# A two-layer decoder trunk on one core: U gathers of layer 1 wait for TensorE, and V rows are placed closer together

## The chip, the cores and the metric

The kernel runs on one core of a Trainium2 chip. The metric is the device time of one execution in microseconds (us). The engines are TensorE (PE, with its weight loads as PEld), VectorE (DVE), ScalarE (ACT), GpSimd (POOL) and SyncE (SP). Each engine works through a queue of its own in order; DMAs are issued from the queues of SP and of POOL.

## The reference, cut to what matters

Two layers, each a token mixer (attention in layer 0, a gated short convolution in layer 1) and then a PEER mixer: for each of 512 tokens a router picks 128 experts (8 heads x 16) out of 16384, each expert being a row of `expert_u` and a row of `expert_v`, of 1024 floats.

```python
for i in range(DEPTH):                      # DEPTH = 2, SEQ = 512, D_MODEL = 1024
    h = rmsnorm(x, norm_mix[i])
    x = x + (sliding_window_attention(h, ...) if i % 2 == 0 else short_gated_conv(h, ...))
    h = rmsnorm(x, norm_ffn[i])
    x = x + peer_ffn(h, peer_w_query[i], peer_sub_keys[i], peer_u[i], peer_v[i])
# in peer_ffn: idx, g = the 128 experts of each token and their softmax weights
u = jnp.take(expert_u, ic, axis=0)
a = jnp.einsum('td,thkd->thk', xc, u)
w = gc * jax.nn.gelu(a, approximate=False)
v = jnp.take(expert_v, ic, axis=0)
y = jnp.einsum('thk,thkd->td', w, v)
```

## The kernel before

The 512 tokens are four tiles of 128. In each layer the PEER mixer is computed in two ways at once. Tiles 2 and 3 are **dense**: all 16384 experts go through TensorE in 128 steps of 128 experts. Step `i` has a key half (`ustep`, L704: load 0.5 MB of transposed U rows as `du`, split them into a high part on ACT, `uh`, and a low part on VectorE, `ul`, 24 matmuls by `mm3`, GELU into `dw`) and a value half (`vstep`, L714: `dw` times the routing weights `G`, split into `wh` and `wl`, load 0.5 MB of V rows as `dv`, split into `vh` and `vl`, 12 matmuls into `y`). The key half runs `LAG` = 7 steps ahead; the first 15 key halves come before step 0, so steps 0 to 7 have a value half alone, and steps 121 to 127 too. `gen` (L738) makes `G` for 32 steps and 16 tokens: ACT copies `jr` and `igr`, VectorE compares and multiplies (`oj`, `igr`, `oi`), 32 small matmuls; 16 gens fill one quarter of the steps. The product `dw` x `G` (L717) runs on GpSimd when it is emitted while U rows are being handed out (`st["gu"]`), else on VectorE.

Tiles 0 and 1 are **gathered** (`gather`, L622): for each of 128 expert places a U gather, an indirect DMA of 128 rows (0.5 MB) issued by POOL (L633), then one VectorE reduction against `xn` (L638); then GELU; then 128 V gathers (L666), each with two matmuls into `acc` (L676). The gather buffers are six (two more in front 1), so a gather waits until the reduction, or the matmul, of an older row has let go of a buffer.

Three streams are written out in one order by `merge` (L814), which has a virtual clock: each `yield` of a stream says how far its next piece lies behind. `stream_d` is the spine: attention of tile 0, front 0 (attention of tiles 1 to 3, router), dense 0, front 1 (`conv` for tiles 1 to 3, projection `proj`, router), dense 1. `stream_g` has the gathers, tile by tile: layer 0 tiles 0 and 1, layer 1 tiles 0 and 1. `stream_f` has the small fronts of the gathered tiles. `rate` (L806) is the distance of two gathered rows on that clock, a pair (U rows, V rows): `DR1` in dense 1, `FR1` in front 1, `DR0` and `FR0` in layer 0. A dense step is `DSTEP` = 6.8, a conv piece 5.25. The order of emission is a priority: a scheduler then puts each engine's queue in order, and it lets an instruction that is ready pass older ones that are not. So a row can run long before the place at which it is emitted.

In front 0 a U row also waits for the last matmul of an attention step that was emitted before it: `attn` sets `st["mark"]` (L341), and `gather` makes the DMA depend on it (L635). In layer 1 there is no mark.

Of the kernel before, what the change touches and what calls it, by code (L numbers as in the profile page):

```python
# [19 lines left out]
P = 128  # L20
D = 1024
KC = 8
# [50 lines left out]
WSB = 2  # L73
GX1 = 2

DR0 = (2.4, 2.4)
DR1 = (2.5, 2.5)
FR0 = (2.2, 3.0)
FR1 = (3.0, 3.0)


@with_exitstack
def trunk(ctx: ExitStack, tc: tile.TileContext, a: dict, out: bass.AP):
    nc = tc.nc
# [25 lines left out]
    first = {}  # L110
# [56 lines left out]
    def split(src, pool, tags, bufs):  # L167
        hi = pool.tile([P, KC, P], F32R, name="whi", tag=tags[0], bufs=bufs)
        lo = pool.tile([P, KC, P], F32R, name="wlo", tag=tags[1], bufs=bufs)
        nc.scalar.copy(hi, src)  # L170
        nc.vector.tensor_tensor(lo, src, hi, op=ALU.subtract)
        return hi, lo

    def mm3(ps, w, x, ts):
        for k in range(KC):
            nc.tensor.matmul(ps, w[0][:, k, :], x[0][:, k, ts], start=(k == 0), stop=False)  # L176
            nc.tensor.matmul(ps, w[0][:, k, :], x[1][:, k, ts], start=False, stop=False)  # L177
        for k in range(KC):
            nc.tensor.matmul(ps, w[1][:, k, :], x[0][:, k, ts], start=False, stop=(k == KC - 1))  # L179

    def proj(src, lhs, tiles, psum, sp):
        for h in range(2):
# [169 lines left out]
    def conv(tiles, pool, psum, slow=1.0):  # L352
        n = len(tiles)
        T = n * P
        gain = gain_of(a["norm_mix"][1:2, :])
        c3 = C3 and n > 1
        if c3:
            hh = pool.tile([P, KC, T], F32R, name="hh", tag="hh")
            hl = pool.tile([P, KC, T], F32R, name="hl", tag="hl")
# [3 lines left out]
        for j, t in enumerate(tiles):  # L363
# [6 lines left out]
            if c3:  # L370
                h = b4.tile([P, D], F32, name="h", tag="b4")
                norm(t, gain, h)
                for half in range(2):
                    ps = psum("psT")
# [16 lines left out]
        for c in range(KC):  # L391
            pss = [None] * 3
            cc = pool.tile([P, 3, T + 2], F32, name="cc", tag="cc")
            u, z, v = cc[:, 0, :T], cc[:, 1, :], cc[:, 2, :T]
            for part in (2, 1, 0):
                w = piece(a["w_in"][c, part])
                ps = psum(f"psbcu{part}")
                if c3:
                    mm3(ps[:, :T], split(w, pool, ("wh", "wl"), WSB), (hh, hl), slice(0, T))
                else:  # L400
                    for k in range(KC):
                        nc.tensor.matmul(ps[:, :T], w[:, k, :], hT[:, k, :], start=(k == 0), stop=(k == KC - 1))
                if part == 2:
                    nc.scalar.copy(u, ps[:, :T])
                elif part == 1:
                    nc.vector.tensor_copy(z[:, 0:2], zh[:, c, :])
                    nc.vector.tensor_tensor(z[:, 2:], ps[:, :T], u, op=ALU.mult)
                    nc.vector.tensor_copy(zh[:, c, :], z[:, T:T + 2])
                    nc.scalar.mul(v, z[:, 0:T], convw[:, 0, c:c + 1])
                    for q in (1, 2):  # L410
                        nc.vector.scalar_tensor_tensor(v, z[:, q:T + q], convw[:, q, c:c + 1], v,
                                                       op0=ALU.mult, op1=ALU.add)
                else:
                    y = v if sp else yT[:, c, :]
                    nc.vector.tensor_tensor(y, v, ps[:, :T], op=ALU.mult)
                    if sp:
                        nc.scalar.copy(yh[:, c, :], y)
                        nc.vector.tensor_tensor(yl[:, c, :], y, yh[:, c, :], op=ALU.subtract)
                yield 1.75 * n * slow
# [202 lines left out]
    def gather(l, t, r):  # L622
# [5 lines left out]
        for s in range(P):  # L628
            if early and s % TK == 0:
                yield f"h{l}_{t}_{s // TK}"  # L630
            h, c = divmod(s, TK)
            ug = gtile("ug")
            ld = nc.gpsimd.indirect_dma_start(out=ug, out_offset=None, in_=a[f"u{l}"],  # L633
                                              in_offset=bass.IndirectOffsetOnAxis(ap=r["idx"][h][:, c:c + 1], axis=0))
            if "mark" in st:  # L635
                tc.add_manual_dep(ld.ins, st["mark"], together, reason="pace of the front")
            with tc.high_priority(offset=HPT):
                nc.vector.tensor_tensor_reduce(out=ug, in0=ug, in1=xn, scale=1.0, scalar=0.0, op0=ALU.mult,  # L638
                                               op1=ALU.add, accum_out=act[:, s:s + 1])
            yield rate()  # L640
# [4 lines left out]
        w = s2.tile([P, P], F32, name="wgt", bufs=1)  # L645
# [7 lines left out]
        for gr in range(2):  # L653
            acc = pv.tile([P, 512], F32, name="acc", tag="acc")
            for q in range(4):
# [5 lines left out]
                for r8 in range(8):  # L661
                    vgs = []
                    for j in range(2):
                        tt = 64 * gr + 32 * j + 8 * q + r8
# [7 lines left out]
                    with tc.high_priority(offset=HPF if st.get("front") else HPV):  # L672
                        for j in range(2):
                            for h in range(2):
                                c = 32 * (2 * j + h)
                                mm = nc.tensor.matmul(acc[c:c + 32, :], wd[:, j, r8, :],  # L676
                                                      vgs[j][:, h * 512:(h + 1) * 512],
                                                      start=(q == 0 and r8 == 0), stop=(q == 3 and r8 == 7))
# [13 lines left out]
    def dense(l, rs, pool):  # L692
        ys = [[py(f"y{tt}{h}") for h in range(2)] for tt in range(2)]
# [20 lines left out]
        def vstep(i):  # L714
            first, last = i == 0, i == NK - 1
            w = ws.pop(i)
            (nc.gpsimd if (WPU if st.get("gu") else WPV) else nc.vector).tensor_tensor(w, w, G[:, i % GR, :], op=ALU.mult)  # L717
            f = VU if st.get("gu") else VG if i % IC >= 2 * IC - GR else VB0
            sp = int((i + 1) * f) > int(i * f)
            if sp:  # L720
                wh = pool.tile([P, T2], F32R, name="wh", tag="wh", bufs=2)
                wl = pool.tile([P, T2], F32R, name="wl", tag="wl", bufs=2)
                nc.scalar.copy(wh, w)
                nc.vector.tensor_tensor(wl, w, wh, op=ALU.subtract)  # L724
            v = pool.tile([P, D], F32, name="dv", tag="raw", bufs=RB)
            nc.sync.dma_start(v, a[f"v{l}"][i * P:(i + 1) * P, :])
            if sp:
                vh, vl = halves(v, [P, D], "v")
                terms = ((wh, vh), (wl, vh), (wh, vl))
            else:  # L730
                terms = ((w, v),)
            for k, (x, m) in enumerate(terms):
                for tt in range(2):
                    for h in range(2):
                        nc.tensor.matmul(ys[tt][h], x[:, tt * P:(tt + 1) * P], m[:, h * 512:(h + 1) * 512],  # L735
                                         start=first and k == 0, stop=last and k == len(terms) - 1)

        def gen(i, tg):  # L738
            ijg = rs[tg * TG // P]["ijg"]
# [29 lines left out]
                gen(c * IC, tg)  # L769

        npre = GR - IC
        for i in range(LAG + npre):
            ustep(i)
            yield 1.0
# [3 lines left out]
        for i in range(NK):  # L778
# [7 lines left out]
            vstep(i)  # L786
            yield DSTEP
        st["ys"] = ys

    def finish(l, ys, pool):  # L790
        for tt in range(2):
# [12 lines left out]
    st = {"dense": False, "front": False, "pace": FS0}  # L804

    def rate():  # L806
        u = 0 if st.get("gu") else 1
        if st["dense"]:
            return (DR1 if "f1" in st else DR0)[u]
        if st["front"]:  # L810
# [182 lines left out]
```

## Time and profile before

| | us |
|---|---|
| median of 3 runs | 2992.05 (2991.13 to 2999.46) |
| the profiled execution | 2989.34 |
| its span, first to last instruction | 2987.5 |
| PE busy | 2624.3 (88%) |
| DVE busy | 2246.6 (75%) |
| ACT busy | 1559.3 (52%) |
| POOL busy | 1364.6 (46%) |

A busy time is a mean over stages that have different limits, so the page is read by stages. On the time axis layer 1 lies so: dense 0 ends about 1655 us, conv's matmuls run from 1675 to 1783, the value halves of dense 1 begin about 2085 and end with the program. U rows of tile 0 are gathered from 1512 to 1808, those of tile 1 from 2077 to 2367; V rows of tile 1 until 2732. In the views a line such as `L735` is a line of the kernel; a count such as x444 is a count of instructions; clock is the granted TensorE clock as a share of the full one.

### The profile page before, as it was taken

The page shows a single profiled execution, that of the slowest core. Times are in us where ns is not written, and L with a number is a line of the kernel's source. Part 1 is how long each engine was busy: PE and PEld are TensorE (multiplying, and loading weights), DVE is VectorE, ACT ScalarE, POOL GpSimd, SP SyncE. Part 2 cuts the span into 40 slices and gives each one's busy share as a digit, 9 for nine tenths or more (in the row PEclk, how much of TensorE's full clock was granted, in tenths as well). Part 3 has the DMA queues.
Part 4 walks back from the last instruction along what each step waited for, and adds up shares of the span by engine and source line. Part 5 has one row for each costly group of instructions (what it writes and reads, how often), then busy time and mean ns, then how long its engine had stood idle before and what let it go on. Part 6 is the DMA issues. An engine that isn't in the chain of part 4 may idle for free. (4 is left out here: it accounts for less than half of the span.)

```text
span 2987.5 us, 53454 instructions
## 1 busy us (share of the span) xinstructions
PE 2624.3 (88%) x19980; PEld 2098.1 (70%) x19980; DVE 2246.6 (75%) x5225; ACT 1559.3 (52%) x2384; POOL 1364.6 (46%) x1163
## 2 busy tenths in 40 slices
PE   5966878869999988999998699986788699999999
PEld 5763476626788877777777696763577577777898
DVE  2496699984898899546479995988999946546655
ACT  4226333584773367448343333358356538637644
POOL 0152554464555545434357754446755755541000
PEclk8987889969999999999999799998899899999999
DMA  5883788989999988999999998998999899996554
GB/s 199 291 315 127 253 311 316 338 315 347 333 367 377 395 304 321 340 324 333 337 366 378 364 366 315 320 335 318 357 348 357 309 338 327 345 333 231 175 187 159
DMA packets 263203, 931.37 MB, mean 312 GB/s; under 512 B 29984, under 2 KB 38560, under 8 KB 262944
## 3 DMA queue, kind: packets, MB, share of 16 engines
q0 software_dynamic: 147456, 536.94, 49.5%
q1 hardware_dynamic: 115488, 391.03, 35.9%
q8 instruction: 157, 2.57, 0.3%
q14 instruction: 102, 0.84, 0.1%
HBM read 916.31 MB, written 11.53 MB: 311 GB/s over the span
## 5 line engine op out<-in xcount | busy, mean ns | idle before, releaser
L633 POOL DMA_INDIRECT ug<-in_u_dram,idx x512 | 684.7, 1337 | 669.6 <-DVE act L638 248.9
L666 POOL DMA_INDIRECT vg<-in_v_dram,idxT x512 | 553.7, 1081 | 640.1 <-PE acc L676 511.8
L638 DVE CUSTOM_DVE_ANT_0 ug<-ug,xn 128x1024 f32<-128x1024 f32 x512 | 626.0, 1235 | 40.0 <-DMA ug<-in_u_dram,idx 39.4
L176 PE MATMUL psA<-xh,uh 128*128 128x256 f32 x2048 | 523.4, 292 | 46.7 <-ACT dw L711 20.0
L177 PE MATMUL psA<-xl,uh 128*128 128x256 f32 x2048 | 510.9, 286 | 0.0
L701 DVE TENSOR_TENSOR ul<-du,uh 128x1024 fp32r<-128x1024 f32 x256 | 320.8, 1253 | 202.7 <-ACT uh L700 163.1
L176 PEld LDWEIGHTS psA<-xh,uh 128*128 128x128 f32 x2048 | 395.4, 193 | 104.9 <-ACT dw L711 32.7
L701 DVE TENSOR_TENSOR vl<-dv,vh 128x1024 fp32r<-128x1024 f32 x256 | 318.5, 1245 | 170.1 <-ACT vh L700 166.6
L177 PEld LDWEIGHTS psA<-xl,uh 128*128 128x128 f32 x2048 | 395.9, 193 | 16.4 <-issue 10.5
L700 ACT CAST uh<-du 128x1024 fp32r<-128x1024 f32 x256 | 268.7, 1050 | 204.7 <-PE psA L177 162.4
L700 ACT CAST vh<-dv 128x1024 fp32r<-128x1024 f32 x256 | 268.9, 1051 | 186.5 <-PE y L735 172.9
L676 PE MATMUL acc<-vg,wd 128*32 128x512 f32 x2048 | 290.4, 646 | 35.4 <-DMA vg<-in_v_dram,idxT 32.1
L179 PE MATMUL psA<-xh,ul 128*128 128x256 f32 x2048 | 299.0, 287 | 18.7 <-DVE ul L701 18.7
L735 PE MATMUL y<-vh,wh 128*128 128x512 f32 x1024 | 289.9, 403 | 27.0 <-ACT vh L700 18.4
L179 PEld LDWEIGHTS psA<-xh,ul 128*128 128x128 f32 x2048 | 266.7, 191 | 52.5 <-DVE ul L701 24.7
L735 PE MATMUL y<-vl,wh 128*128 128x512 f32 x1024 | 287.5, 402 | 16.0 <-DVE vl L701 15.7
L735 PE MATMUL y<-vh,wl 128*128 128x512 f32 x1024 | 283.2, 397 | 16.6 <-DVE wl L724 16.5
L742 ACT COPY jr<-ijg 128x2048 f16<-128x2048 f16 x128 | 243.5, 1902 | 50.6 <-DVE oj L746 49.7
L735 PEld LDWEIGHTS y<-vh,wl 128*128 128x128 f32 x1024 | 192.8, 190 | 73.1 <-DVE wl L724 20.8
L735 PEld LDWEIGHTS y<-vl,wh 128*128 128x128 f32 x1024 | 189.1, 191 | 72.4 <-DVE vl L701 21.2
L735 PEld LDWEIGHTS y<-vh,wh 128*128 128x128 f32 x1024 | 178.6, 191 | 73.8 <-ACT vh L700 25.6
L744 ACT COPY igr<-ijg 128x1536 f16<-128x1536 f16 x128 | 188.8, 1475 | 35.3 <-DVE oi L751 34.9
(208 smaller groups left out, 4004.8 us busy)
## 6 DMA issues: line engine op xcount, KB each, us to landing
du<-in_uT_dram SPq DMA_DIRECT2D x256, 512.0 KB, 6.5
dv<-in_v_dram SPq DMA_DIRECT2D x256, 512.0 KB, 6.3
wpc<-in_wq_dram SPq DMA_DIRECT2D x64, 512.0 KB, 6.0
wpc<-in_w_in_dram SPq DMA_DIRECT2D x48, 512.0 KB, 7.1
wpo<-in_wo_dram SPq DMA_DIRECT2D x16, 512.0 KB, 4.5
ug<-in_u_dram,idx POOLq DMA_INDIRECT x512, 7.6
vg<-in_v_dram,idxT POOLq DMA_INDIRECT x512, 7.2
wpo<-in_w_out_dram SPq DMA_DIRECT2D x16, 512.0 KB, 6.7
```

The source lines that it names most:

```text
L176: nc.tensor.matmul(ps, w[0][:, k, :], x[0][:, k, ts], start=(k == 0), stop=False)
L177: nc.tensor.matmul(ps, w[0][:, k, :], x[1][:, k, ts], start=False, stop=False)
L179: nc.tensor.matmul(ps, w[1][:, k, :], x[0][:, k, ts], start=False, stop=(k == KC - 1))
L633: ld = nc.gpsimd.indirect_dma_start(out=ug, out_offset=None, in_=a[f"u{l}"], in_offset=bass.IndirectOffsetOnAxis(ap=r["idx"][h][:, c:c + 1 ...
L638: nc.vector.tensor_tensor_reduce(out=ug, in0=ug, in1=xn, scale=1.0, scalar=0.0, op0=ALU.mult, op1=ALU.add, accum_out=act[:, s:s + 1])
L666: ld = nc.gpsimd.indirect_dma_start(out=vg, out_offset=None, in_=a[f"v{l}"], in_offset=bass.IndirectOffsetOnAxis(ap=idxT[:, tt:tt + 1], ax ...
L676: mm = nc.tensor.matmul(acc[c:c + 32, :], wd[:, j, r8, :], vgs[j][:, h * 512:(h + 1) * 512], start=(q == 0 and r8 == 0), stop=(q == 3 and ...
L700: nc.scalar.copy(hi, w)
L701: nc.vector.tensor_tensor(lo, w, hi, op=ALU.subtract)
L735: nc.tensor.matmul(ys[tt][h], x[:, tt * P:(tt + 1) * P], m[:, h * 512:(h + 1) * 512], start=first and k == 0, stop=last and k == len(terms ...
L742: nc.scalar.copy(jr, ijg[:, 0, t0:t0 + TG].unsqueeze(2).to_broadcast([P, TG, P]))
L744: nc.scalar.copy(igr, ijg[:, 1:4, t0:t0 + TG].unsqueeze(3).to_broadcast([P, 3, TG, IC]))
```

## The change

In conv for tiles 1 to 3, every piece's last matmul becomes the mark. In dense 1 the mark at the time a row is emitted is the last matmul of the value half one step before the one just emitted. So a U gather of layer 1 that is emitted behind the first conv piece waits, on POOL, for the mark that holds at its emission; U rows of tile 0 that are emitted before it have none. V gathers wait for no mark. The distances change too: V rows of dense 1 from 2.5 to 1.8, U rows of front 1 from 3.0 to 3.5, V rows of front 1 from 3.0 to 2.5. U rows of dense 1 stay at 2.5, which is 6.8 / 2.5 = 2.7 rows to a step.

```diff
-DR1 = (2.5, 2.5)
+DR1 = (2.5, 1.8)
-FR1 = (3.0, 3.0)
+FR1 = (3.5, 2.5)
...
 def mm3(ps, w, x, ts):
...
-            nc.tensor.matmul(ps, w[1][:, k, :], x[0][:, k, ts], start=False, stop=(k == KC - 1))
+            mm = nc.tensor.matmul(ps, w[1][:, k, :], x[0][:, k, ts], start=False, stop=(k == KC - 1))
+        return mm.ins.name
...
 def conv(tiles, pool, psum, slow=1.0):
...
-                    mm3(ps[:, :T], split(w, pool, ("wh", "wl"), WSB), (hh, hl), slice(0, T))
+                    st["mark"] = mm3(ps[:, :T], split(w, pool, ("wh", "wl"), WSB), (hh, hl), slice(0, T))
...
 def gather(l, t, r):
...
-            if "mark" in st:
+            if st.get("mark"):
                 tc.add_manual_dep(ld.ins, st["mark"], together, reason="pace of the front")
...
 def dense(l, rs, pool):
     def vstep(i):
...
-                        nc.tensor.matmul(ys[tt][h], x[:, tt * P:(tt + 1) * P], m[:, h * 512:(h + 1) * 512],
-                                         start=first and k == 0, stop=last and k == len(terms) - 1)
+                        mm = nc.tensor.matmul(ys[tt][h], x[:, tt * P:(tt + 1) * P], m[:, h * 512:(h + 1) * 512],
+                                              start=first and k == 0, stop=last and k == len(terms) - 1)
+            if l == 1:
+                st["mark"], st["next"] = st["next"], mm.ins.name
...
         npre = GR - IC
+        st["mark"] = st["next"] = None
         for i in range(LAG + npre):
...
         st["ys"] = ys
+        st["mark"] = st["next"]
```

## Rows read from the trace of the kernel before

**Rows 1.** Windows of dense 1: length, busy us (instructions) of each engine, clock, DMA.
```profile
2085.00:2385.00 300.00, 226.86 (x1662) 188.56 (x1663) 293.86 (x455) 163.80 (x209) 202.88 (x143) 0.91 0.92 340
2385.00:2732.00 347.00, 347.00 (x2767) 258.68 (x2769) 185.92 (x213) 194.25 (x263) 164.48 (x163) 1.00 0.92 330
```
**Rows 2.** The chain that ended last: start us, us, what.
```profile
2389.85 2.71 PE acc L676 x24
...
2943.05 2.77 PE y L735 x12
2948.66 2.77 PE y L735 x12
```
**Rows 3.** Windows of three lines alone: L735 twice, L179 once, L755 twice.
```profile
2085.00:2385.00 300.00, 122.19 (x444) 85.28 (x444) 0.91 0.92 340
2385.00:2732.00 347.00, 140.38 (x552) 98.85 (x552) 1.00 0.92 330
...
2085.00:2385.00 300.00, 33.30 (x232) 30.31 (x232) 0.91 0.92 340
...
2085.00:2385.00 300.00, 15.66 (x512) 14.10 (x512) 0.91 0.92 340
2385.00:2732.00 347.00, 20.16 (x608) 17.17 (x608) 1.00 0.92 330
```
**Rows 4.** Window of tile vg: PE, PEld and POOL; four matmul records to a row.
```profile
2385.00:2732.00 347.00, 66.89 (x508) 10.28 (x512) 126.58 (x122) 1.00 0.92 330
```
**Rows 5.** Windows of the seam and of the projection, columns as in rows 1.
```profile
1597.00:1655.00 58.00, 43.57 (x231) 36.19 (x229) 56.98 (x84) 21.00 (x30) 45.89 (x32) 0.97 0.96 358
1650.00:1675.00 25.00, 5.63 (x24) 4.71 (x24) 23.13 (x41) 7.93 (x15) 16.50 (x14) 0.52 1.01 396
1785.00:1860.00 75.00, 68.16 (x406) 47.72 (x406) 42.08 (x104) 26.56 (x42) 32.85 (x32) 0.95 0.87 320
```
**Rows 6.** Tiles ug, psbcu, vg: duration ns min/median/max, first and last start us.
```profile
L633 POOL DMA_INDIRECT ug<-in_u_dram,idx x68: 933/1234/1987, 1511.7 to 1659.6; - x68
...
L179 PE MATMUL psbcu<-hh,wlo x192: 336/336/339, 1683.4 to 1782.8; 128*128 128x384 f32 x192
...
L676 PE MATMUL acc<-vg,wd x512: 589/617/1064, 1820.5 to 2083.2; 128*32 128x512 f32 x171
```
**Rows 7.** Window of tile ug: DVE and POOL.
```profile
1650.00:1675.00 25.00, 13.45 (x12) 16.50 (x14) 0.52 1.01 396
```
**Rows 8.** Lines of DVE, 2100 to 2340: xcount, busy us, mean ns, idle before.
```profile
L638 DVE CUSTOM_DVE_ANT_0 ug<-ug,xn 128x1024 f32<-128x1024 f32 x108 | 129.3, 1215 | 1.3 <-DMA ug<-in_u_dram,idx 1.3
...
L701 DVE TENSOR_TENSOR ul<-du,uh 128x1024 fp32r<-128x1024 f32 x26 | 31.8, 1224 | 1.4 <-ACT uh L700 1.4
L746 DVE TENSOR_TENSOR oj<-jr,io 128x2048 f16<-128x2048 f16 x14 | 17.2, 1226 | 0.0
L724 DVE TENSOR_TENSOR wl<-dw,wh 128x256 fp32r<-128x256 f32 x24 | 10.0, 415 | 0.1
L751 DVE TENSOR_TENSOR oi<-igr 128x1024 f16<-128x1024 f16 x14 | 9.6, 682 | 0.0
...
L749 DVE TENSOR_TENSOR igr<-igr,io 128x512 f16<-128x512 f16 x13 | 5.4, 412 | 0.0
```
**Rows 9.** Lines of DVE and POOL, 2345 to 2358.
```profile
L638 DVE CUSTOM_DVE_ANT_0 ug<-ug,xn 128x1024 f32<-128x1024 f32 x5 | 8.2, 1641 | 0.0
...
L724 DVE TENSOR_TENSOR wl<-dw,wh 128x256 fp32r<-128x256 f32 x2 | 1.9, 946 | 0.0
...
L717 POOL TENSOR_TENSOR dw<-dw,G 128x256 f32<-128x256 f32 x9 | 11.4, 1299 | 0.0
```
**Rows 10.** Reductions and waits (us, times, longest): 240 to 460, then 2085 to 2385.
```profile
L638 DVE CUSTOM_DVE_ANT_0 ug<-ug,xn x74: 1198/1217/1226, 265.9 to 456.6; 128x1024 f32<-128x1024 f32 x74
...
  DMA ug<-in_u_dram,idx: 25.6, 19
...
DVE ug L638 <- DMA ug<-in_u_dram,idx: 5.9, 6, 2.0
```

## The prediction

> **What bounds the kernel now.** I read the page's slices first: where TensorE's digits dip, VectorE's go to 9, so no one engine sets the pace throughout. Then come the windows of dense 1, cut where the gathers of tile 1 change from U rows to V rows. From 2085 to 2385 us VectorE is busy 293.9 of 300 us; from 2385 to 2732 it is busy 185.9 of 347, and TensorE all the time [rows 1].
>
> TensorE's busy time is modelled, so I count its work instead. In the bare tail the chain of work has a whole dense step in 2948.66 - 2943.05 = 5.61 us, of which the value half is 2.77 us; that leaves 2.84 for the key half (`ustep`). A gathered V row costs 2.71 / 6 = 0.45 us (24 matmuls are 6 rows) [rows 2]. In the U stage 444 / 12 = 37 value halves, 232 / 8 = 29 key halves and 512 / 32 = 16 gens ran [rows 3]: 102 + 82 + 16 = 200 us of work in 300, so **TensorE idles 100 us**. In the V stage 46 value halves, as many key halves, 19 gens (1.06 us each) and 127 rows [rows 3, 4] are 127 + 131 + 20 + 57 = 335 of 347: 12 us idle. The V stage is TensorE's; the U stage is VectorE's. All that a better spread can win in dense 1 lies in those 100 us.
>
> A second place is the seam between dense 0 and front 1. From 1597 to 1655 us TensorE lacks 58 - 43.6 = 14.4 us, and from 1650 to 1675, at a granted clock of 0.52 (mostly the lower of its levels, 1.2 of 2.4 GHz), it lacks 19.4 of 25; VectorE is at 57.0 of 58 and 23.1 of 25 [rows 5].
>
> **The change, part by part.** Rows are handed out by `merge`, whose virtual clock can be worked through by hand from the yields. Before, the 128 U rows of (layer 1, tile 1) have places from step 31 to step 78 of dense 1, but nothing holds them there: they ran in the first 37 steps, 128 / 37 = 3.5 to a step. After, V rows of tile 0 end at step 24 in that order (2.5 and 1.8 in place of 3.0 and 2.5), U rows of tile 1 have places in steps 24 to 71 (47 steps, 2.7 each), and now each waits for the value half one step before its own. V rows of tile 1 have steps 71 to 105, with no wait.
> For tile 0 of layer 1, rows 0 to 38 stand ahead of the first conv piece and wait for nothing; rows 39 to 74 wait for the pieces, 1.5 to a piece; the last 53 wait for the last piece alone.
>
> *1. The seam.* The 68 U rows issued from 1511.7 to 1659.6 us were 2.2 us apart, so row 39 went out about 1597; now it waits for the first conv piece, which ended about 1685 [rows 6]. Some 40 reductions leave VectorE there. The last steps of dense 0 then need about 2 us of VectorE (vl, wl, dw) against 2.77 of TensorE, so most of the 14.4 us goes: -11, bounds -14 and 0. In the 25 us before conv, 12 reductions are 13.5 us of VectorE [rows 7] between the links of the norm chain: -10, bounds -13 and -3. Together -21.
>
> *2. Conv, projection and router.* Conv is dense with matmuls and has fewer rows beside it: 0. Its last piece ended about 1783 [rows 6], with item 1 about 1765, and then the last 53 rows come, freed together: 65 us of VectorE at 1.22 each, to about 1765 + 53 x 2.2 = 1882. From 1785 to 1860 VectorE has 75 - 42 = 33 us free [rows 5]; over 95 us that is 42, so some 20 us reach into the router or wait. Against it, 42 V rows (below) leave front 1 and with them 19 us of TensorE, which is busy 68.2 of 75 there [rows 5]. Half of the second against a third of the first: -3, bounds -19 and +20.
>
> *3. V rows that move into dense 1.* The V rows of tile 0 had their matmuls from 1820.5 to 2083.2 us, 2.05 a row [rows 6]. Beginning about 1888, they end about 2151; dense 1's value halves start about 2085 - 21 = 2064, so 42 rows are left then: 42 x 0.45 = +19, bounds 0 and +25. Step 24 comes at 2064 + 8 x 2.77 + 16 x 5.61 + 13 gens + 19 + 12 idle = 2220, so they are done in time; POOL then has a hole of some 70 us, for which no one waits.
>
> *4. The U stage over 47 steps.* VectorE's sum, by its lines [rows 8]: 128 x 1.22 = 156; 47 x (1.22 + 1.22 + 0.42) = 134 for vl, ul, wl; 18 gens x (1.23 + 0.68 + 0.41) = 42. `dw` is POOL's in these steps (before it was VectorE's in steps 0 to 31). While nine of them ran back to back, reductions took 1.64 us and wl 0.95 [rows 9], for 1.22 and 0.42 alone [rows 8]: five reductions, two wl and three gen operations were stretched by about 0.5 each, 4.8 us in all, 0.53 for each dw. That is the upper end, zero the lower; I take 0.3 (a dw doesn't always meet such an operation): 14 us. The stage is 346 us. TensorE's work in it: 47 x 5.61 + 18 = 282. Idle 64 in place of 100: **-36**, bounds -50 and -25. The first 24 steps, which are now outside it, get an idle time like the V stage's: +12, bounds +5 and +20.
>
> The stretch just read bears on a rule of the Trainium skill, page "SBUF — State Buffer", section "SBUF: two separate sides": a VectorE operation with two SBUF inputs and a GpSimd operation that reads SBUF take a shared port pair as an exclusive lock, and the loser blocks for the whole instruction. By that rule each dw would cost VectorE its whole time; the stretched rows show less than that, 0.53.
>
> *5. The price of the wait.* A row is issued only when its step allows, so a reduction can reach the head of VectorE's queue before its row has landed; behind it stand ul, vl and wl, and TensorE waits for those. The nearest gated rows are those of front 0, which wait for attention matmuls: 25.6 us in 19 waits for 74 rows, 0.35 a row; the ungated rows of dense 1 cost 5.9 us in 6 waits [rows 10]. For 128 rows that is 44 us, so bounds 0 and +38. I take 0.15 a row, +13: dense 1 holds its VectorE queue fuller than front 0, so a row has longer to land. On POOL a dw stands behind gated rows; TensorE has 8.5 us (key, value, key half) before it is needed, and three issues at a median of 1.23 [rows 6] and a dw fit in that: 0.
>
> *6. The end.* The U stage ends about 2220 + 346 = 2566; the V rows took 347 us [rows 4], so to about 2913. From step 71 TensorE has 50 x 5.61 + 7 x 2.77 + 58 (rows) + 16 (gens) + 12 = 386 us, to 2952: some 40 us in hand, and at 3.0 us a row none. 0, bounds 0 and +15.
>
> **Sum:** -21 - 3 + 19 - 36 + 12 + 13 = **-16**. The profiled execution took 2989.3 us (span 2987.5), 2.7 under the median of 2992.05; I take the difference to the median: **2976 us**.
>
> **The rivals.**
> A. *Landing waits take the place of the starved stage* (slower). If the first row of each gated step waits the mean of front 0's waits, 25.6 / 19 = 1.35 us [rows 10], the price is 47 x 1.35 = 63 instead of 19: -16 + 44 = +28, 3020 us. It decides from about 44 us of such waits in dense 1 (0.94 a step), where the sum reaches +9. For it: it is the one price seen of gated rows here. Against: attention has a lighter VectorE queue.
> B. *The stall only moves* (same). VectorE does the same reductions, and the U stage is VectorE's before and after; with the stage at its upper bound (-25 in place of -36) the sum is -5: 2987 us.
> C. *dw on POOL locks VectorE for its full length*: 11.4 / 9 = 1.27 us by the rows at their slowest [rows 9], so 47 x 1.27 = 60 instead of 14: -16 + 46 = +30, 3022 us. It decides from 0.85 a dw. The skill's page on SBUF named above states such a lock. Against: reductions went on at 1.64 us through that very stretch.
> D. *More comes back*: the seam gives its -27, landing costs nothing, dw nothing: -16 - 6 - 13 - 14 = -49, 2943 us. For it: nine dw ran together at 2345 [rows 9] because they had stood on POOL behind U rows; with gated rows POOL has time for them early.
>
> **How the numbers follow.** Forecast 0.40 (of it 0.05 within 9 us of 2992), D 0.15, B 0.22, A 0.18, C 0.05. A measurement of this kernel tells about 0.3%, 9 us, from no change. Faster: 0.35 + 0.15 = 0.50. Same: 0.05 + 0.22 = 0.27. Slower: 0.18 + 0.05 = 0.23. The range 2940 to 3014 takes in D's time, B and the lower ends of A and C; it leaves out the rest of A and C (some 0.13) and the outer piece of D. The faster cases alone would have 2940 to 2983.
>
> **What would show it.** The U reductions of tile 1 should lie about 2220 to 2566, 2.7 to a step; if they begin near 2080 as before, the wait does not do what it says. Windows over the seam should show TensorE's idle 34 us down to about 13. TensorE's work counted in the U stage should be about 282 of 346 us. Waits of reductions for their rows in dense 1: 19 us by the forecast, 63 by A. Reductions in the U stage near 1.3 us by the forecast, 1.6 by C. The forecast is wrong if the U stage takes over 370 us, if V rows outlast the dense steps, or if router 1 ends later than dense 0's gain brings it forward.

## The result, and the profile after

The changed kernel took 3015.31 us (median of 4 runs, 3011.37 to 3024.26) against 2992.41 for the kernel before on the same chip: a ratio of 1.0076, 95% interval 1.0052 to 1.0100. It is slower by 23 us, and just outside the range given. On a second chip (run e9 below) it was 2997.62 against 2986.65, a ratio of 1.0046 [1.0027, 1.0064]. The two intervals meet from 1.0052 to 1.0064. (A ratio here and below is the estimate on record with its 95% interval; it can differ from the quotient of the two medians by up to 0.0012.)

The profiled execution of the first runs took 3024.26 us (span 3022.5) and was the longest of its four. That of e9 took 2996.76 us (span 2995.0), 0.9 under its median. So sizes are taken from e9's trace where the two differ, and both are shown. Line numbers are one higher than before from L180 on, three higher in the gens (L758 for L755).

The two waits stand where the prediction put them. This is tile `ug`, `psbcu` and `vg` of the changed kernel, first profile (answers to rows 6; columns as there; the second and the last line are tile 1):

```profile
L634 POOL DMA_INDIRECT ug<-in_u_dram,idx x128: 932/1305/2006, 1519.0 to 1880.8; - x128
L634 POOL DMA_INDIRECT ug<-in_u_dram,idx x128: 933/1407/1992, 2262.6 to 2625.8; - x128
...
L179 PE MATMUL psbcu<-hh,wlo x192: 333/336/445, 1677.0 to 1773.8; 128*128 128x384 f32 x192
...
L677 PE MATMUL acc<-vg,wd x512: 589/617/1063, 1909.4 to 2193.4; 128*32 128x512 f32 x171
L677 PE MATMUL acc<-vg,wd x512: 589/593/617, 2640.1 to 2990.3; 128*32 128x512 f32 x171
```

U rows of tile 1 now begin 144 us behind the first value half of dense 1 (2118.3) and spread over the next 363; before they began at its start. U rows of tile 0 end at 1881 in place of 1808.

Windows of dense 1 of the changed kernel, U stage and V stage, all engines (answers to rows 1, columns as there), then the U stage for L736, L179 and L758 alone (answers to rows 3):

```profile
2262.50:2637.00 374.50, 320.79 (x2533) 277.43 (x2530) 351.57 (x484) 225.20 (x294) 240.28 (x175) 0.95 0.87 320
2637.00:2993.00 356.00, 352.47 (x2688) 261.87 (x2688) 182.78 (x238) 177.91 (x253) 131.74 (x129) 1.00 0.92 330
...
2262.50:2637.00 374.50, 153.44 (x588) 107.55 (x588) 0.95 0.87 320
...
2262.50:2637.00 374.50, 58.04 (x392) 52.07 (x392) 0.95 0.87 320
...
2262.50:2637.00 374.50, 22.98 (x760) 20.72 (x756) 0.95 0.87 320
```

The U stage holds 588 / 12 = 49 value halves, 392 / 8 = 49 key halves and 24 gens: 49 x 5.61 + 24 x 1.06 = 300 us of TensorE work in 374, so 74 idle. VectorE is still its bound, 351.6 of 374.5.

So the U stage does not explain a loss. The whole program, cut at events that each trace shows (the first U gather of layer 1, the last matmul of dense 0 into `y`, the first and last conv matmul, the first matmul of the gens, the first value half of dense 1, the end of the span), says where the time went. All lengths in us; the last two columns count the U reductions, and VectorE's busy time, from conv's last matmul to the first gen:

| kernel | ratio to before | to dense 0's end | seam | conv | conv to first gen | gens to dense 1 | dense 1 to end | U reductions | VectorE |
|---|---|---|---|---|---|---|---|---|---|
| before | 1 | 134.3 | 29.1 | 107.7 | 216.0 | 91.0 | 897.7 | 7 | 165.5 |
| changed, first | 1.0076 | 130.7 | 21.6 | 102.5 | 245.5 | 99.0 | 904.2 | 58 | 229.8 |
| changed, e9 | 1.0046 | 128.9 | 21.5 | 100.6 | 241.3 | 91.8 | 898.8 | 58 | 228.8 |
| e3 distances only | 0.9985 | 132.8 | 28.5 | 108.5 | 216.7 | 90.8 | 895.0 | 7 | 165.5 |
| e1 dense wait only | 0.9965 | 132.7 | 28.8 | 108.4 | 220.0 | 89.3 | 886.0 | 7 | 167.1 |
| e7 dense wait, early rows | 0.9965 | 132.9 | 28.4 | 107.3 | 201.8 | 110.8 | 888.6 | 7 | 151.4 |
| e2 conv wait only | 1.0045 | 128.9 | 20.9 | 101.5 | 239.3 | 92.3 | 910.1 | 57 | 228.2 |
| e6 short reductions | 0.9977 | 128.9 | 20.6 | 102.8 | 211.4 | 96.4 | 916.4 | 58 | 167.7 |
| e5 | 1.0011 | 128.8 | 22.0 | 103.4 | 216.1 | 108.2 | 907.6 | 47 | 204.6 |
| e8 | 0.9976 | 128.9 | 22.4 | 102.2 | 223.3 | 96.5 | 899.3 | 46 | 214.2 |
| e4 old distances | 0.9972 | 129.0 | 20.2 | 101.0 | 230.7 | 84.1 | 904.8 | 52 | 226.2 |
| e11 | 1.0015 | 128.9 | 21.2 | 101.1 | 231.7 | 84.0 | 913.0 | 52 | 226.1 |
| e10 | 1.0036 | 128.9 | 20.8 | 105.6 | 239.7 | 81.5 | 909.6 | 51 | 232.0 |
| e12 | 0.9981 | 128.9 | 20.4 | 102.0 | 224.2 | 84.9 | 907.9 | 49 | 220.7 |

From before to e9: -5.4 - 7.6 - 7.1 + 25.3 + 0.8 + 1.1 = +7; the spans differ by 7.5 (by 35 with the first profile). The 11 us between the medians are these 7.5, the 2.7 by which the profiled execution of before lies above the median of before beside e9, and the 0.9 by which e9's own lies under its median. The gain before and beside conv is 20 us, the loss behind it 26, in the changed kernel's first profile 37.

The loss, read in windows (all engines, columns as in rows 1), from conv's last matmul to the first gen, each followed by the same window for tile `ug` alone (VectorE, GpSimd). Before:

```profile
1782.80:1998.80 216.00, 200.34 (x1438) 150.47 (x1438) 165.50 (x732) 91.98 (x168) 94.01 (x94) 0.96 0.89 321
...
1782.80:1998.80 216.00, 8.54 (x7) 4.89 (x5) 0.96 0.89 321
```

The changed kernel, first profile:

```profile
1773.80:2019.30 245.50, 201.49 (x1401) 164.88 (x1401) 229.80 (x878) 92.41 (x171) 141.65 (x114) 0.92 0.91 333
...
1773.80:2019.30 245.50, 69.35 (x58) 78.23 (x55) 0.92 0.91 333
```

The same kernel in e9:

```profile
1763.10:2004.40 241.30, 198.39 (x1401) 162.85 (x1400) 228.78 (x878) 92.48 (x171) 141.11 (x114) 0.92 0.93 339
...
1763.10:2004.40 241.30, 68.43 (x58) 77.95 (x55) 0.92 0.93 339
```

TensorE is busy there as long as before, to 2 us, and idle for 43 us in e9 in place of 16, so neither its work nor its clock (0.92 for 0.96) sets the length. VectorE has 51 more reductions, 60 us of them, and goes from 165.5 of 216 (77%) to 228.8 of 241.3 (95%). Router 1 needs VectorE for its selection of experts, and the gens need the router. The cast into `ijg`, with which the router's result for a tile is ready (first and last start), in before, then in e9:

```profile
L521 DVE CAST ijg<-psi x2: 400/407/414, 1979.6 to 2002.8; 128x256 f16<-128x256 f32 x2
```

```profile
L522 DVE CAST ijg<-psi x2: 407/412/416, 1984.5 to 2009.0; 128x256 f16<-128x256 f32 x2
```

Conv ended 20 us earlier in e9 (1763.1 for 1782.8), and the router 5 us later: 221 us behind conv in place of 197.

How the held rows come to land there is seen in tile `ug` by 25 us windows (VectorE, GpSimd; clock, DMA share, GB/s). Before:

```profile
1600.00:1625.00 25.00, 13.72 (x11) 16.18 (x12) 1.00 1.02 387
1625.00:1650.00 25.00, 14.78 (x13) 18.41 (x13) 1.00 0.90 333
1650.00:1675.00 25.00, 13.45 (x12) 16.50 (x14) 0.52 1.01 396
1675.00:1700.00 25.00, 17.43 (x16) 20.73 (x15) 0.87 0.90 332
1700.00:1725.00 25.00, 15.09 (x13) 18.64 (x14) 0.93 1.03 408
1725.00:1750.00 25.00, 14.20 (x12) 15.99 (x13) 1.00 1.00 384
1750.00:1775.00 25.00, 13.71 (x13) 10.87 (x8) 1.00 0.98 371
...
1800.00:1825.00 25.00, 6.07 (x5) 2.81 (x3) 0.93 0.80 266
1825.00:1850.00 25.00, 0.00 (x0) 0.00 (x0) 0.93 0.99 383
```

The changed kernel, e9:

```profile
1600.00:1625.00 25.00, 6.50 (x6) 1.19 (x1) 1.00 0.74 253
1625.00:1650.00 25.00, 0.00 (x0) 0.00 (x0) 0.87 0.40 144
1650.00:1675.00 25.00, 0.00 (x0) 3.94 (x3) 0.79 0.20 71
1675.00:1700.00 25.00, 11.99 (x10) 10.89 (x9) 1.00 0.87 307
1700.00:1725.00 25.00, 9.97 (x10) 12.44 (x9) 1.00 0.91 306
1725.00:1750.00 25.00, 10.87 (x9) 11.84 (x9) 1.00 0.91 313
1750.00:1775.00 25.00, 11.16 (x11) 14.96 (x12) 1.00 0.91 327
...
1800.00:1825.00 25.00, 14.61 (x14) 15.46 (x13) 0.59 0.94 372
1825.00:1850.00 25.00, 14.38 (x12) 20.73 (x15) 1.00 0.95 345
```

In the three windows from 1600 to 1675, 36 reductions before are 6 after. Beside conv the rows then run at 9 to 11 to a window, slower than before (12 to 16), so none of the 30 is made good there, and 14 more are lost from 1675 to 1775 (54 before, 40 after). The DMA engines, at 0.90 to 1.03 before, are at 0.40 and 0.20 in the hole. In these 75 us POOL issued 4 gathers in place of 39, and behind conv the rows came at the old pace of about 2 us each (14 and 12 to a window).

### The profile page after: what moved, and what is told of

It reads as the page before. It is cut to its first block, busy times and chain, and to the rows that moved or that the text cites. A ratio compares the mean times of both kernels' runs of the same rounds, so it can differ in the third digit from the quotient of the medians.

```text
span 3022.5 us, 53433 instructions
## 1 busy us (share of the span) xinstructions
PE 2640.0 (87%) x19980; PEld 2102.5 (70%) x19980; DVE 2251.8 (75%) x5225; ACT 1556.0 (51%) x2383; POOL 1382.6 (46%) x1163
## 5 line engine op out<-in xcount | busy, mean ns | idle before, releaser
L639 DVE CUSTOM_DVE_ANT_0 ug<-ug,xn 128x1024 f32<-128x1024 f32 x512 | 632.8, 1246 | 55.6 <-DMA ug<-in_u_dram,idx 53.6
L179 PE MATMUL psA<-xh,ul 128*128 128x256 f32 x2048 | 299.8, 288 | 24.3 <-DVE ul L702 23.8
L179 PEld LDWEIGHTS psA<-xh,ul 128*128 128x128 f32 x2048 | 266.6, 191 | 62.4 <-DVE ul L702 32.1
L736 PE MATMUL y<-vl,wh 128*128 128x512 f32 x1024 | 287.5, 402 | 18.7 <-DVE vl L702 18.4
L736 PE MATMUL y<-vh,wh 128*128 128x512 f32 x1024 | 288.4, 402 | 12.8 <-ACT vh L701 11.9
L736 PE MATMUL y<-vh,wl 128*128 128x512 f32 x1024 | 281.7, 395 | 3.5 <-DVE wl L725 3.5
L736 PEld LDWEIGHTS y<-vl,wh 128*128 128x128 f32 x1024 | 188.1, 191 | 77.6 <-DVE vl L702 25.1
L736 PEld LDWEIGHTS y<-vh,wl 128*128 128x128 f32 x1024 | 191.9, 189 | 59.0 <-issue 10.7
L736 PEld LDWEIGHTS y<-vh,wh 128*128 128x128 f32 x1024 | 178.2, 190 | 65.8 <-ACT vh L701 20.3
L749 DVE TENSOR_TENSOR oj<-jr,io 128x2048 f16<-128x2048 f16 x128 | 158.3, 1237 | 70.3 <-PE acc L677 16.2
```

What stands on the lines that cost most here:

```text
L179: mm = nc.tensor.matmul(ps, w[1][:, k, :], x[0][:, k, ts], start=False, stop=(k == KC - 1))
L736: mm = nc.tensor.matmul(ys[tt][h], x[:, tt * P:(tt + 1) * P], m[:, h * 512:(h + 1) * 512], start=first and k == 0, stop=last and k == len( ...
L749: nc.vector.tensor_tensor(oj, jr, io128.unsqueeze(1).to_broadcast([P, TG, P]), op=ALU.is_equal)
```

## The experiments

**Which part does it.** The theory before these runs: the waits of conv send rows behind it onto a VectorE without room (loss), the dense wait works as forecast. The rival: the loss is in dense 1, by V rows or by landing waits. Three kernels have one part each.

e1, only the wait in dense 1 (and the new distances):

```diff
-                    st["mark"] = mm3(ps[:, :T], split(w, pool, ("wh", "wl"), WSB), (hh, hl), slice(0, T))
+                    mm3(ps[:, :T], split(w, pool, ("wh", "wl"), WSB), (hh, hl), slice(0, T))
```

> The changed kernel without the conv marks: only the U rows of tile 1 wait for dense steps, the distances are the new ones. Theory F (front): the 23 us are lost between the end of conv and the first value half of dense 1 (1774 to 2118 us in the changed kernel, 344 us; 1783 to 2090 before, 307 us), because the 53 U rows of tile 0 held back behind conv run beside the projection and the router and push the V rows into the gens of dense 1. Without conv marks that stretch is about 307 us again, the first value half comes at about 2090, dense 1 takes about 895, and the time is 2975 to 2997. Rival W (waits in dense 1): the loss comes from gated rows in dense 1; then this kernel keeps it, 3010 or more. Rival R (any new order costs this much): 3000 to 3015 with the loss in another place.

Measured: 2977.84 against 2987.56, ratio 0.9965 [0.9954, 0.9977]. Dense 1 to the end is 886.0 us, 9 less than with the distances alone (e3, 895.0); no stage ahead of dense 1 differs from e3 by more than 3.3 us. The dense wait gains 9 us by these two profiles and 5.5 by the medians (2977.84 against e3's 2983.32); the two intervals still touch. Beside the conv waits the gain doesn't show in the time: 1.0045 without the dense wait (e2), 1.0046 and 1.0076 with it.

e2, only the waits in conv:

```diff
-                st["mark"], st["next"] = st["next"], mm.ins.name
+                st["next"] = None
```

> The changed kernel without the dense marks: U rows of tile 0 wait for conv's pieces, those of tile 1 for nothing. Theory F: conv end to first value half about 340 us as in the changed kernel, first value half about 2115, and a time of 3005 to 3025. Rival W: 2985 to 2997, as before the change.

Measured: 3003.34, ratio 1.0045 [1.0028, 1.0062], just under the expected 3005. Seam and conv give back 15 us against e3 (20.9 and 101.5 for 28.5 and 108.5) and dense 0's end 4; the stretch from conv to dense 1 is 331.6 for 307.5, and dense 1 to the end 910.1 for 895.0. At these distances the loss belongs to the conv waits: 20 us by the medians of e2 and e3.

e3 has both edits above, so no wait in layer 1 and the new distances alone.

> No marks at all in layer 1, only the new distances (2.5, 1.8) and (3.5, 2.5). Theory F: rows without marks run as soon as a buffer is free, wherever they are emitted, so the time is within 10 us of 2992 and conv end to first value half about 307 us. Rival R: over 3000 although nothing waits.

Measured: 2983.32, ratio 0.9985 [0.9972, 0.9997]. The distances alone cost nothing.

**e4, both waits with the old distances:**

```diff
-DR1 = (2.5, 1.8)
+DR1 = (2.5, 2.5)
-FR1 = (3.5, 2.5)
+FR1 = (3.0, 3.0)
```

> Both kinds of marks with the old distances (2.5, 2.5) and (3.0, 3.0). U rows of tile 1 then have steps 31 to 78 of dense 1 instead of 24 to 71. Theory F: the front loses less than in the changed kernel, since at 3.0 more U rows of tile 0 (46 instead of 36) go beside conv and fewer (about 45) behind it; but V rows of tile 1 begin at step 78 and last 350 us, so they outlast the dense steps by 10 to 30 us: 3010 to 3040. If V rows are closed up by the scheduler at the end: 3000.

Measured: 2982.89, ratio 0.9972 [0.9955, 0.9988]. V rows of tile 1 had their last matmul at 2973.1, after the last of dense 1 at 2963.5, so with this distance they do outlast the dense steps. The expected 3010 to 3040 is missed: the kernel is a little faster than before, and 0.7 to 1% faster than the changed one: 52 instead of 58 rows behind conv, and 314.8 us from conv to dense 1 instead of 333 (e9). The distances, harmless without the waits, matter with them.

**e6, the disputed cost by itself.** The changed kernel with the reductions of places 75 to 127 of layer 1, tile 0, cut to 64 columns: gathers, buffers, waits and the order of emission stay, and VectorE loses the length of those 53 reductions. This leaves out the rest of these dot products.

```diff
+                n = 64 if (l, t) == (1, 0) and s >= 75 else D
-                nc.vector.tensor_tensor_reduce(out=ug, in0=ug, in1=xn, ...
+                nc.vector.tensor_tensor_reduce(out=ug[:, :n], in0=ug[:, :n], in1=xn[:, :n], ...
```

> The changed kernel with one cost taken out: the reductions of the U rows of tile 0 that are emitted behind conv's last piece (places 75 to 127, 53 rows) run over 64 columns instead of 1024, so the mixer's output for these places is not computed; their gathers are unchanged. It takes some 53 x 1.05 = 56 us from VectorE. Theory V: the stretch from the end of conv to the first value half falls from 344 to 300 to 320 us, and the time to 2975 to 2995. Rival G, or one in which the gathers themselves (DMA, POOL) hold up the front: the stretch stays over 330, the time over 3005.

Measured: 2992.33 against 2997.15, ratio 0.9977 [0.9961, 0.9994], for 1.0076 and 1.0046 with full reductions. Windows of e6 as above, whole and tile `ug`, and the router's end:

```profile
1764.00:1975.40 211.40, 176.72 (x1215) 150.04 (x1214) 167.68 (x817) 86.13 (x161) 95.72 (x90) 0.94 0.88 326
...
1764.00:1975.40 211.40, 16.90 (x58) 58.97 (x55) 0.94 0.88 326
...
L522 DVE CAST ijg<-psi x2: 411/414/418, 1958.0 to 1982.1; 128x256 f16<-128x256 f32 x2
```

The same 58 rows arrive in the stretch, at 17 us of VectorE instead of 68. VectorE is back at 167.7, the router ends 194 us behind conv (before 197, e9 221), and the stretch is 211.4 us (before 216.0). So it is VectorE's time for these rows that the changed kernel pays there, not the number of their gathers or the waits. (POOL's share shrank with it: the same 55 issues took 59 us for 78 in e9.) Part of the 25 us comes back later: dense 1 to the end took 916.4 us, 17.6 more than in e9, since 52 V rows of tile 0 were left for dense 1 in place of 30, which is 10 us of TensorE at 0.45 a row; the rest isn't explained. The ratio keeps 0.7% against e9 (across two chips).

**Can the rows be placed better?** e5 hands out front 1's rows closer, so that fewer are left for the end of conv; e7 and e8 do so with early U rows in dense 1 too, e7 without the conv waits.

```diff
-FR1 = (3.5, 2.5)
+FR1 = (2.5, 2.5)
```

> The changed kernel with the distances of front 1 at (2.5, 2.5): 50 instead of 36 U rows of tile 0 are let go beside conv, so about 37 instead of 53 stand behind its last piece; U rows of tile 1 have steps 14 to 61 instead of 24 to 71. Theory V (VectorE is full from the projection to the gens, and every row behind conv adds its 1.2 us there): the stretch from the end of conv to the first value half, 344 us in the changed kernel and 315 with 3.0, falls to 305 to 318, conv itself gains less than the 6 us it gained; time 2970 to 2990. Rival G (the V rows that come later hold up the gens, however many U rows went before them): the stretch stays at 325 or more, time over 2995.

Measured: 3000.88 against 2997.15, ratio 1.0011 [0.9995, 1.0027]. 47 rows in place of 58, and the first gen comes 216.1 us behind conv, as before. But from there to dense 1 it takes 108.2, and the whole is 324.3. The expectation of theory V (305 to 318, under 2990 us) is missed, and the numbers lie at the bounds of rival G (325, 2995), though before itself took 2997 on this chip. Part of it is that work which had stood ahead of the first gen (TensorE was busy 168 of those 216 us, in e9 198 of 241) now stood behind it. Rival G as the whole cause is answered by e6 alone.

```diff
-DR1 = (2.5, 1.8)
+DR1 = (3.0, 1.8)
-FR1 = (3.5, 2.5)
+FR1 = (2.0, 2.0)
-                    st["mark"] = mm3(...)
+                    mm3(...)
```

> Dense marks only, none in conv, with distances that let the U rows of tile 1 begin at step 5 of dense 1, where V rows of tile 0 really end, and spread them over 56 steps (2.3 rows to a step) instead of 47: DR1 = (3.0, 1.8), FR1 = (2.0, 2.0). If VectorE's share of a step is what TensorE idles for in the U stage, 9 more steps take 9 x 2.7 = 24 us of idle time, less some 10 for the steps before 24 that were free of rows: the dense stage takes 860 to 872 us (878 with dense marks at the distances of the change, 887 without), time 2960 to 2975. If gating costs as much as it gives, 2975 to 2990.

Measured: 2985.68, ratio 0.9965 [0.9947, 0.9982], as e1: the first gen comes 14 us earlier than in before, and 20 us more lie between it and dense 1. Dense 1 to the end took 888.6 us, so the wider spread didn't bring the 860 to 872 that were hoped for.

e8 keeps the conv waits, with `DR1 = (3.0, 1.8)` and `FR1 = (2.4, 2.2)`.

> Both kinds of marks, DR1 = (3.0, 1.8), FR1 = (2.4, 2.2): 53 U rows of tile 0 beside conv, some 34 behind it; U rows of tile 1 in steps 11 to 67. Theory V: the seam and conv keep their gain of 14 us, the stretch behind conv is 305 to 318 us (307 before), the V rows that move into dense 1 cost about 15 there, and the spread gives 15 to 25: time 2960 to 2980. Rival G: over 2985.

Measured: 2988.43, ratio 0.9976 [0.9961, 0.9992]; 46 rows, 319.8 us from conv to dense 1; both that and the time miss theory V (318, 2980), and the time is in rival G's range. e5 and e8 leave 47 and 46 rows behind conv and differ by 0.35%, and e4 with 52 has the shorter stretch (314.8). So the count of late rows alone doesn't order these kernels; what the distances do besides isn't settled by these runs.

**The changed kernel again, and an earlier mark.** e9 is the changed kernel again.

> The changed kernel once more, for a second profiled execution (the first was the slowest of its four). Theory (a full VectorE behind conv sets the loss): the stretch from conv's last matmul to the first value half of dense 1 is again 330 to 350 us (before 307), with 55 to 60 U reductions between conv's last matmul and the first matmul of the gens and VectorE at 93 to 98% there, and the ratio is 1.004 to 1.011. Rival (the first profile showed a chance execution, and the loss lies elsewhere): the stretch is 307 to 320 us while the ratio is still over 1.004.

Measured: as in the table; 333.1 us from conv to dense 1, 58 rows, VectorE at 95%. The first profile was a long execution of the same pattern.

e10 makes marks of the first four of conv's eight chunks alone, so that later rows are let go in the middle of conv:

```diff
-                    st["mark"] = mm3(ps[:, :T], split(w, pool, ("wh", "wl"), WSB), (hh, hl), slice(0, T))
+                    last = mm3(ps[:, :T], split(w, pool, ("wh", "wl"), WSB), (hh, hl), slice(0, T))
+                    if c < 4:
+                        st["mark"] = last
```

> The changed kernel, but only the pieces of the first four of conv's eight chunks become marks, so that rows emitted later wait for a piece in the middle of conv and not for the last. Theory (what costs is that the held rows are let go behind conv): the seam keeps 20 to 24 us (before 29, changed 22), 20 to 40 U reductions lie between conv's last matmul and the first gen matmul in place of 58, the stretch behind conv is 305 to 320 us, and the ratio to the kernel before is 0.990 to 0.998. Rival (holding rows against conv costs as much wherever they are let go): the ratio stays at 1.004 or above and the stretch at 330 or more. Second rival (the held rows come out of conv instead): conv's matmuls take 110 us or more in place of 102.

Measured: 2995.81 against 2986.65, ratio 1.0036 [1.0025, 1.0047]. The theory missed its numbers: not 20 to 40 rows behind conv but 51, and 321.2 us where 305 to 320 were expected. The first rival (330 or more) and the second (110 us of conv, measured 105.6) miss too: against e9 the stretch is 12 us shorter, conv 5 and dense 1 to the end 11 us longer, and the ratio the same within its interval. Why so many rows are still late is in the same windows of tile `ug`, here e10 from 1700 to 1775:

```profile
1700.00:1725.00 25.00, 10.96 (x9) 16.06 (x13) 1.00 0.92 335
1725.00:1750.00 25.00, 14.34 (x12) 17.54 (x14) 1.00 1.03 409
1750.00:1775.00 25.00, 15.05 (x13) 15.50 (x13) 1.00 1.01 396
```

Let go early, the rows come at 9 to 13 to a window, with the DMA engines at 1.01 to 1.03 when they come at 12 and 13: the old pace and not a faster one. So the 30 rows of the hole were not made good beside conv here either, though they waited for an earlier piece. That ending the hole still sooner would not help is argued from this pace, not shown.

e11 is the changed kernel with the old front distances, `FR1 = (3.0, 3.0)`; e12 has e10's edit and all old distances.

> The changed kernel with the distances of front 1 as before, (3.0, 3.0) in place of (3.5, 2.5); V rows of dense 1 stay at 1.8. It stands between the changed kernel (1.0076) and both waits with all old distances (0.9972). Theory (rows let go behind conv): 50 to 54 U reductions in that stretch instead of 58, the stretch 312 to 325 us, ratio 0.996 to 1.001. Rival (the V distance of dense 1, 2.5 to 1.8, is what costs): ratio 1.005 or above, with the stretch as in the changed kernel or the dense steps 10 us longer than the 885 with old distances.

Measured: 2992.23, ratio 1.0015 [1.0001, 1.0028]; 52 rows, 315.7 us from conv to dense 1, dense 1 to the end 913.0. The expected 1.001 is missed by a hair, and the row between e9 and e4 is split: the front distances give 0.3%, the V distance in dense 1 the rest (0.4%, across two chips). In which step of dense 1 the latter lies isn't shown: to the program's end it took 904.8 with the old distance (e4) and 913.0, 904.2 and 898.8 with the new (e11 and the two profiles of the changed kernel).

> Both waits and all old distances, and only the first four of conv's eight chunks as marks. Theory: as with both waits and old distances (0.9972), less what the rows behind conv cost there (52 rows, about 8 us): ratio 0.991 to 0.997, stretch behind conv 303 to 315 us, seam 20 to 24. Rival (no loss was left behind conv with the old distances): ratio 0.997 or above, and V rows again end at the last dense steps.

Measured: 2980.99, ratio 0.9981 [0.9969, 0.9993]; 49 rows, 309.1 us. The stretch is as expected, the time is the rival's: it is no better than e4 without the early mark (0.9972), and in both the last V row ends behind the last dense step (here 2966.9 against 2956.3). With the same hole and 49 late rows this kernel lost only 2 us behind conv (309.1 for 307.0), so late rows need not cost that much; with the distances of the change 58 of them did. Neither kernel beats the dense wait alone: **e1 and e7, at 0.9965, have the lowest ratio here**, though e4's interval overlaps theirs.

## Why the prediction was wrong, step by step

**Item 1, the seam (-21): right in kind, 13 us of it; that the sum fits is luck.** Windows of before and of e9 over the last 51 us of dense 0 and from there to conv (all engines, columns as in rows 1; they answer to rows 5), before first:

```profile
1595.00:1646.00 51.00, 44.09 (x233) 36.70 (x232) 49.98 (x71) 19.01 (x28) 40.25 (x28) 1.00 0.97 368
1646.00:1675.00 29.00, 6.06 (x26) 4.71 (x24) 27.13 (x49) 9.92 (x17) 19.60 (x16) 0.59 0.98 376
```

```profile
1590.00:1641.00 51.00, 47.06 (x259) 40.18 (x257) 37.02 (x49) 21.21 (x31) 13.20 (x11) 1.00 0.61 215
1641.00:1663.00 22.00, 6.21 (x27) 5.33 (x26) 12.90 (x21) 9.91 (x18) 0.00 (x0) 0.63 0.38 143
```

VectorE falls from 50 to 37 and from 27 to 13 us, as foreseen. TensorE's idle time goes from 6.9 + 22.9 to 3.9 + 15.8, so 10 us of the 21. In the table dense 0's end and the seam together take 149 to 152 us in every kernel with conv waits and 161 to 163 in the four without: 13 us from before to e9. Conv itself, booked at 0, gives 7 more, for a reason no run isolates. Together 20, near the forecast by the one error making up for the other.

**Item 2, conv, projection and router (-3): this is the step that failed.** It measured +26 (e9) and +37 (first profile), and +24 with the conv waits alone (e2 against e3), beyond its upper bound of +20. The facts in it were right: 53 rows at the end of conv, 2.2 us apart, to about 1882 (measured 1881, and 1869 in e9). Wrong was the weight. It took the some 20 us of reductions that reach into the router at one third, and set them against one half of the 19 us of TensorE time of departed V rows. No row stood behind either share, and the 20 us in full, its upper bound, were still too few. From conv's end to the first gen VectorE was busy 165.5 of 216 us in before, so it had 50.5 us free, and 51 reductions more are 60. The V rows that left gave TensorE nothing it could use, since the router's VectorE operations came last. Over the stretch from conv to dense 1 VectorE's busy time rose by 55 us (247.7 to 302.7), of which 29 went into free time and 26 into the end: half of the 59 us that had been free stayed unused. The window of 75 us that was read [rows 5] showed the free time but not who waits for the engine at its end; the router's own selection stood past it.

**Item 3, V rows moved into dense 1 (+19): right within its bounds.** 98 of the 128 V rows of tile 0 were done before dense 1 began, so 30 moved, not 42; 13.5 us of TensorE. With conv waits dense 1 to the end is 15 us longer without the dense wait (e2 against e3) and 13 and 18 with it (e9 and the first profile against e1).

**Item 4, the U stage (-36 + 12), with item 5 (+13): right in sum, -9 for -11 (-5.5 by the medians of e1 and e3).** The U stage took 373 us in e9, over the 370 that was named as a sign of error: two more steps and 24 gens rather than 18 stand in it, and its idle time is 73 us, landing waits included, for 64 + 13. The idle of the steps ahead of it is 5 to 9 us instead of 12. Idle time of TensorE in dense 1 by the same count of work falls from 114 (before) to 102 (e1).

**Item 5, landing waits (+13): right; rival A falls.** DVE's waits in dense 1 of the changed kernel (answers to rows 10), and what POOL waited for ahead of `ug` in the same stage:

```profile
DVE ug L639 <- DMA ug<-in_u_dram,idx: 15.8, 13, 2.5
...
  PE y L736: 73.8, 31
```

15.8 us in 13 waits, 17.2 in 15 in e9: the forecast was 19, rival A's price 63. POOL does wait for the steps, 73.8 us, and as item 5 said hardly anyone is late for a `dw` behind it: in the U stage ACT waits 3.4 us for POOL's `dw`, TensorE never.

**Rival C falls.** DVE's and POOL's lines, 2270 to 2620 us of the changed kernel (answers to rows 8 and 9):

```profile
L639 DVE CUSTOM_DVE_ANT_0 ug<-ug,xn 128x1024 f32<-128x1024 f32 x120 | 153.1, 1288 | 15.4 <-DMA ug<-in_u_dram,idx 14.8 <-issue 0.3
L702 DVE TENSOR_TENSOR ul<-du,uh 128x1024 fp32r<-128x1024 f32 x46 | 58.1, 1263 | 1.5 <-ACT uh L701 1.5
...
L749 DVE TENSOR_TENSOR oj<-jr,io 128x2048 f16<-128x2048 f16 x23 | 29.6, 1287 | 2.8 <-PE psG L758 2.8
L725 DVE TENSOR_TENSOR wl<-dw,wh 128x256 fp32r<-128x256 f32 x47 | 23.7, 504 | 0.0
L754 DVE TENSOR_TENSOR oi<-igr 128x1024 f16<-128x1024 f16 x23 | 17.8, 776 | 0.1
...
L718 POOL TENSOR_TENSOR dw<-dw,G 128x256 f32<-128x256 f32 x41 | 44.4, 1094 | 30.8 <-ACT dw L712 14.5 <-ACT G L765 13.1 <-DVE vl L702 2.1
```

A reduction is 1.29 us (1.22 alone), `oj` 1.29 (1.23), `oi` 0.78 (0.68), `wl` 0.50 (0.42), `ul` 1.26 (1.22). These surpluses, times their counts, are 8.8 + 1.4 + 2.2 + 4.2 + 1.8, and with `vl` (1.24 for 1.22) and `igr` (0.46 for 0.41) some 20 us over 41 `dw`, about 0.50 for each; 0.3 was taken, 0.53 was the upper end, and the rival needed 0.85 to decide and 1.27 in full.

The means hide the shape. A line of POOL and two of DVE from the timeline of the same stretch (start us, us):

```profile
2403.69 0.90 POOL L718 TENSOR_TENSOR dw<-dw,G 128x256 f32<-128x256 f32 x1
...
2403.92 1.75 DVE L639 CUSTOM_DVE_ANT_0 ug<-ug,xn 128x1024 f32<-128x1024 f32 x1
...
2405.60 1.22 DVE L639 CUSTOM_DVE_ANT_0 ug<-ug,xn 128x1024 f32<-128x1024 f32 x1
```

An operation of VectorE is not stretched a little each time: from 2270 to 2620, 37 are longer than the rest of their kind, nearly all by 0.52 to 0.58 us whatever their own length, and each of the 37 overlaps a `dw`. So the surplus goes with `dw`, though no run here took `dw` away. (The 1.64 us of the prediction was such a mean too: four of its five reductions took 1.74 to 1.76, one 1.21.)

By the rule of the Trainium skill that the prediction weighed (page "SBUF — State Buffer", section "SBUF: two separate sides") the operation that starts first has the shared pair for its whole instruction, and the other blocks. The all-or-nothing 0.53 us fits a lock, but it is half of a `dw`'s recorded 1.09; how much of that length is `dw`'s own waiting no run here shows.

**Item 6, the end (0): right.** V rows end at 2990.3, 32 us ahead of the end of the span (also in e9), for 40 foreseen.

**The sum with the one term put right:** -16 + 3 + 26 = +13, and with the first profile's 37, +24; measured were 11 (e9) and 23 (7 and 35 by the spans). Rival B had the thought, that VectorE does the same reductions and the stall only moves, but priced it in dense 1, where the change gained, and not in the stretch behind conv. Of the signs named, two came true: the U stage over 370 us, which cost nothing in sum (item 4), and "router 1 ends later than dense 0's gain brings it forward", which is the loss.

## What to carry to other kernels

Work held back from one stage must be priced in the stage that it lands in: take the busy time of the engine up to the next event that waits for it, not over a window cut short. And don't count its free time there in full. Of 59 us free behind conv the late rows filled 29 in e9 and 43 in e12, and why the distances make that difference isn't settled. A hold also leaves a hole in the transfers: here 30 rows, which neither e9 nor e10 made good beside conv. And try the parts of a change alone: here one wait by itself gained 5 to 9 us, the other lost 20.

## What the runs showed of the hardware beyond this

TensorE's granted clock fell in a stretch in which the changed kernel holds no row back. Windows from the first gen to the first value half of dense 1 (all engines; the third value from the end is the clock), before and then the changed kernel's first profile:

```profile
1998.80:2089.80 91.00, 65.11 (x894) 39.75 (x892) 82.21 (x296) 78.94 (x86) 56.79 (x50) 0.88 0.91 325
```

```profile
2019.30:2118.30 99.00, 61.46 (x778) 28.45 (x777) 72.49 (x251) 74.27 (x75) 52.91 (x49) 0.74 0.83 287
```

From 0.88 to 0.74 (0.77 in e9, 0.69 in e11), so more of the stretch lay at the lower of its levels, 1.2 of 2.4 GHz. TensorE was busy 61 of 99 us there, and 65 of 91 before. The stretches with the lowest clock are not the longest (e11: 84.0 us), so what the clock cost isn't read from these runs.
